# An encoder layer's last projection, moved behind all gated projections and written as a 2x2 block product with seven multiplications

## The chip, the core and the metric

The kernel runs on one core of one Trainium2 chip. The metric is the time of one execution on the device, in microseconds (us). Smaller is better. Three runs of the kernel before took 2499.37, 2503.11 and 2503.69 us; their median is 2503.11 us.

The engines are named as the profile names them: PE does matrix multiplications (PEld loads their stationary operand), DVE is the vector engine, ACT the scalar engine, POOL is GpSimd, SP issues most transfers. PE adds into banks of PSUM; everything else lies in SBUF or in DRAM.

## What is computed

The layer works on two inputs x of 1024 rows by 1024 channels each (one prompt, one sample). It ends so:

```
y_f = (fz * silu(fg)) @ w_fourier_out
y_h = (z * silu(hg)) @ w_hyena_out
g_f, g_h = split(sigmoid(mg + b_merge))
out = (g_f * y_f + g_h * y_h) @ w_out
return x + rmsnorm(out, g_post)
```

All matrices there are 1024x1024 in float32. Each operand of a multiplication is split into a rounded part h and a rest l, and a product is h*h + h*l + l*h: three passes of PE. Only the last projection, `@ w_out`, and what feeds it are changed.

## The kernel before, in words

**Stages.** `phase_fourier` and `phase_main` compute the Fourier and the Hyena branch. `phase_gates` (L956) computes the rest of the gate columns of x1 @ w_in. `phase_out` (L1066) does the two output projections, the merge and the last projection.

**How phase_gates multiplies.** It writes a product as 2x2 blocks, with Winograd's form of seven block products in place of eight. A job is one pair of 128-column blocks of w_in: `prepare` (L964) loads four 128x512 pieces by POOL's queue into two buffers "raw", and DVE and ACT make the sums s1 to s4 and split everything. `times` (L1011) is one block product: 12 matmuls of 128x512. The seven are named by their left operand: 11, 12, s2, s3, s1, s4, 22. Some add into the same PSUM bank: 11, then s2, then s1, then s4 all go into `pa`, and ACT copies the bank to SBUF (`kept`, L1034) between them. So a product into `pa` has to wait until the copy of the one before is done. The next job's 11 and 12 stand between this job's s1 and s4.

**How phase_out works.** A unit is one half (512 rows) of one input: four units. For each unit:
- f: eight products `pyf` (L1105, one for each 128 output channels, 24 matmuls each), times the sigmoid gate (`gated`, L1114), giving `yf`;
- h: eight products `pyh`, gated and added to `yf`. The sum is the operand of the last projection, `M`; ACT and DVE split it into `mh` and `ml`, which stay in SBUF;
- out: four row tiles of 128 rows by 1024 columns, `po`: 2 x 24 matmuls each, with `M` as the stationary and w_out as the moving operand. ACT squares `po` and sums it, DVE multiplies by g_post, `rstd` (L232, a chain of small DVE operations) and a multiply-add with x give the output rows.

The operands of f and h are tiles `sf` and `sh` (`operand`, L1078), 256 KB each, loaded by SP's queue into the places of the split x (`xh`, `xl`), and split by ACT and DVE. The weights of f and h stream through POOL's queue (`weight`, L1092): 128x512 pieces in three buffers, two of the pool `wp` and one of `op`, each loaded, split and used for 12 matmuls. w_out is loaded in unit 0 (`load_wo`, L1123) between the f products, 16 pieces of 256 KB, split as they come and kept.

**What sets the order.** The program is put in order by a scheduler that works from its own times; every engine and every queue then runs its instructions strictly in that order, and each waits for its semaphores at its turn. An instruction that waits holds up all behind it on the same engine. `keep_in_program_order` pins the first matmul of a block product. `tc.issue_after` puts DMA issues behind a named instruction. A pool's buffers are reused in turn (`bufs`), and a tile may be written only when the last reader of its place is done; pools opened later in a stage take the places of pools of the stage before.

Of the kernel before, what the change touches and what calls it, by code (L numbers as in the profile page):

```python
# [16 lines left out]
P = 128  # L17
D = 1024
# [143 lines left out]
class K:  # L162
# [34 lines left out]
    def setup(self, ctx):  # L197
# [27 lines left out]
        self.d_g = [{s: [dt(f"d_g{b}_{s}_{k}", [P, L]) for k in range(8)] for s in (0, 4, 5, 6)} for b in range(NB)]  # L225
        self.d_w = [[[dt(f"d_w{s}_{k}_{i}", [P, L]) for i in range(2)] for k in range(8)] for s in range(3)]
        self.d_sh = [[dt(f"d_sh{b}_{k}", [P, L]) for k in range(8)] for b in range(NB)]

# [721 lines left out]


    PLAIN = [(5, 0), (5, 1), (6, 0), (6, 1), (5, 2), (5, 3), (6, 2), (6, 3), (5, 4), (5, 5)]

    def phase_gates(self):
# [6 lines left out]
        with ExitStack() as es:  # L961
# [29 lines left out]
            A = prepare(*jobs[0])  # L991

            TH, TL = [], []
            for k in range(4):
                r = gr.tile([P, 4, 512], F32, tag="raw", name="xraw", bufs=2)
                for i in range(2):
                    nc.sync.dma_start(r[:, 2 * i:2 * i + 2].rearrange("p a b -> p (a b)"), self.d_x[b][k + 4 * i])
                s = gw.tile([P, 4, 512], F32, tag="sum", name="xsum", bufs=1)
                self.sub("dve", s[:, 0::2], r[:, 0:2], r[:, 1::2])
                self.stt("dve", s[:, 1], s[:, 0], -1.0, r[:, 3], MUL, SUB)  # L1000
                self.add("dve", s[:, 3], s[:, 1], r[:, 2])
# [7 lines left out]
            T1, T2, T3, T4 = [[(TH[k][:, j], TL[k][:, j]) for k in range(4)] for j in range(4)]  # L1009

            def times(p, A, B, first):  # L1011
                for k in range(4):
                    h, l = A[0][:, k], A[1][:, k]
                    for j, (w, x) in enumerate(((h, B[k][0]), (h, B[k][1]), (l, B[k][0]))):
                        m = self.mm(p, w, x, first and k + j == 0, k + j == 5, True)
                        if k + j == 0:
                            tc.keep_in_program_order(m)

# [15 lines left out]
            def kept(p, own=False):  # L1034
                t = gw.tile([P, 512], F32, tag="u", name="u", bufs=1) if own else wp.tile([P, 512], F32, tag="w", name="m", bufs=2)
                nc.scalar.copy(t, p)
                return t

            def first(A):
                pa, pb = self.psum("mm", 4, "pg"), self.psum("X", 2, "pg")  # L1040
                times(pa, A["11"], B11, True)
                m1 = kept(pa)
                times(pb, A["12"], B21, True)
                return pa, pb, m1
            pa, pb, m1 = first(A)
            for i, (sec, c) in enumerate(jobs):
                out(sec, c, 0, pb, m1, ADD)
                times(pa, A["s2"], T2, False)
                u = kept(pa, True)
                pc = self.psum("T", 2, "pg")  # L1050
                times(pc, A["s3"], T3, True)
                times(pa, A["s1"], T1, False)
                v = kept(pa)
                out(sec, c + 1, 1, pc, v, SUB)
                last = (A, pa, pc, u)
                if i + 1 < len(jobs):
                    A = prepare(*jobs[i + 1])
                    pa, pb, m1 = first(A)
                A_, pa_, pc_, u = last
                times(pa_, A_["s4"], B22, False)  # L1060
                out(sec, c, 1, pa_, None, None)
                times(pc_, A_["22"], T4, False)
                out(sec, c + 1, 0, pc_, u, SUB)


    def phase_out(self):  # L1066


# [3 lines left out]
        with ExitStack() as es:  # L1072
            pool = lambda n: es.enter_context(tc.tile_pool(name=n, bufs=1, reuse_waits="tile"))
            oc, sp, op, ox = pool("oc"), pool("sp"), pool("op"), pool("ox")
            wo = {}
# [38 lines left out]
            def gated(i, dt, ps, sec, bias, out):  # L1114
                b, half = units[i]
                g = wp.tile([P, 512], F32, tag="gt", name="g", bufs=3)
                nc.sync.dma_start(g, self.d_g[b][sec][dt][:, 512 * half:512 * half + 512])
                nc.scalar.activation(g, g, AF.Sigmoid, bias=self.bm[:, bias:bias + 1])
# [3 lines left out]

            def load_wo(k):  # L1123
                wo[k] = [oc.tile([P, D], F32R, tag=f"{t}{k}", name=f"{t}{k}", bufs=1) for t in ("woh", "wol")]
                for n in range(2):
                    s = slice(512 * n, 512 * n + 512)
                    r = wp.tile([P, 512], F32, tag="gt", name="wor", bufs=3)
                    nc.sync.dma_start(r, a["w_out"][k * P:(k + 1) * P, s])
                    self.split(wo[k][0][:, s], wo[k][1][:, s], r, "dve", "act")

            S = {(0, "f"): [operand(0, "f", k) for k in range(8)]}
            gp = oc.tile([P, D], F32, name="gp")
            nc.sync.dma_start(gp, a["g_post"][0].partition_broadcast(P))
            for i, (b, half) in enumerate(units):
                Yf, M = [], []
                S[i, "h"] = []
                for dt in range(8):
                    ps = project(i, "f", "w_fo", dt, S[i, "f"])
                    S[i, "h"].append(operand(i, "h", dt))
                    if i == 0:  # L1140
                        load_wo(dt)
                    y = sp.tile([P, 512], F32, tag=f"ml{dt}", name=f"yf{dt}", bufs=1)
                    Yf.append(gated(i, dt, ps, 5, dt, y))
                S[i + 1, "f"] = []
                for dt in range(8):
# [4 lines left out]
                    self.add("dve", g, Yf[dt], g)  # L1150
                    mh = sp.tile([P, 512], F32R, tag=f"mh{dt}", name=f"mh{dt}", bufs=1)
                    ml = sp.tile([P, 512], F32R, tag=f"ml{dt}", name=f"ml{dt}", bufs=1)
                    self.split(mh, ml, g, "dve", "act")
                    M.append((mh, ml))
                for tt in range(4):
                    c = slice(P * tt, P * tt + P)
                    row = 512 * half + P * tt
                    x = ox.tile([P, D], F32, tag="x", name="xr", bufs=2)
                    nc.sync.dma_start(x, a[f"x{b}"][row:row + P, :])
                    ss = op.tile([P, 2], F32, tag="ss", name="ss", bufs=2)  # L1160
                    s1 = op.tile([P, 1], F32, tag="s1", name="s1", bufs=2)
                    rs = op.tile([P, 1], F32, tag="rs", name="rs", bufs=2)
                    ps = [self.psum("mm", 4, f"po{n}") if tt < 2 else self.psum(("X", "T")[n], 2, f"po{n}")
                          for n in range(2)]
                    o = ox.tile([P, D], F32, tag="o", name="o", bufs=2)
                    for n in range(2):
                        s = slice(512 * n, 512 * n + 512)
                        for k in range(8):
                            self.mm3(ps[n], (M[k][0][:, c], M[k][1][:, c]), (wo[k][0][:, s], wo[k][1][:, s]),
                                     k == 0, k == 7)  # L1170
                        sq = op.tile([P, 512], F32, tag="sq", name="sq", bufs=1)
                        nc.scalar.activation(sq, ps[n], AF.Square, accum_out=ss[:, n:n + 1])
                        self.mul("dve", o[:, s], ps[n], gp[:, s])
                    nc.vector.tensor_tensor(s1, ss[:, 0:1], ss[:, 1:2], op=ADD)
                    self.rstd(op, rs, s1, 1)
                    for n in range(2):
                        s = slice(512 * n, 512 * n + 512)
                        self.stt("dve", o[:, s], o[:, s], rs, x[:, s], MUL, ADD)
                        nc.sync.dma_start(a[f"y{b}"][row:row + P, s], o[:, s])

# [79 lines left out]
```

## Time and profile before

| | |
|---|---|
| median of three runs | 2503.11 us |
| the profiled execution | 2505.81 us |
| its span, first to last instruction | 2504.0 us |
| PE busy | 2432.6 us, 97%, 13280 matmuls |
| DVE busy | 1906.1 us, 76% |
| ACT busy | 1067.9 us, 43% |
| POOL busy | 465.6 us, 19% |
| mean DMA rate | 163 GB/s |
| `po` matmuls | 768, in four stretches between 2028 and 2495 us |

How to read it: a matmul record of 128x512 is 0.389 us long, but a new one starts every 0.2267 us, since they are pipelined; so PE's work is counted by the distance of starts. Idle time "<-" names what ended it. The granted clock is the share of full TensorE clock.

### The profile page before, as it was taken

The numbers are of one execution on the slowest core, as the hardware profiler recorded it, in microseconds if no ns is written. First come the engines' busy times: TensorE is split into PE (matmuls) and PEld (weight loads), VectorE is DVE, ScalarE is ACT, GpSimd is POOL, SyncE is SP. The second block draws the span as 40 slices with busy tenths as digits, with TensorE's granted clock in tenths as the row PEclk, the third lists the DMA queues.
The fourth block names the chain that finished last, engine by engine and source line by source line (L and its number), as shares of the span: only waits on it lengthen the run. The fifth ranks groups of instructions, "written<-read, shape, count | busy, mean of one in ns | idle before, by whom it ended". The sixth has DMA issues, their size and how long they took to land.

```text
span 2504.0 us, 37217 instructions
## 1 busy us (share of the span) xinstructions
PE 2432.6 (97%) x13280; PEld 2106.1 (84%) x13280; DVE 1906.1 (76%) x3719; ACT 1067.9 (43%) x2000; POOL 465.6 (19%) x482
## 2 busy tenths in 40 slices
PE   6999999999999999999999999999999999999998
PEld 6988888888878888888888888887888778888887
DVE  7686788888788999999889999976655564545444
ACT  6546666666643333333323323323433552424241
POOL 1331222222233433440000001212000110101010
PEclk9999999999999999999999999999999999999999
DMA  7636555555555555546444443434454763545441
GB/s 270 200 105 220 195 162 163 157 171 163 172 183 179 178 170 163 175 145 210 127 136 133 135 144 127 148 127 168 160 181 133 246 218 122 188 136 173 146 144 51
DMA packets 204945, 408.40 MB, mean 163 GB/s; under 512 B 22662, under 2 KB 69991, under 8 KB 204376
## 3 DMA queue, kind: packets, MB, share of 16 engines
q1 hardware_dynamic: 180252, 319.71, 39.5%
q0 software_dynamic: 24320, 86.31, 10.1%
q8 instruction: 104, 1.70, 0.3%
q14 instruction: 81, 0.66, 0.1%
q10 hardware_dynamic: 188, 0.02, 0.0%
HBM read 280.11 MB, written 125.83 MB: 162 GB/s over the span
## 4 chain that ended last, share of the span: by engine, by line
PE 46%; DMA 5%; DVE 2%; issue 1%; ACT 1%; SPq 0%; DVEq 0%; POOL 0%; ACTq 0%; POOLq 0%
PE pin L194 13%; PE pg L194 8%; PE po L194 6%; PE pyf L194 5%; PE pyh L194 5%; PE pT L194 4%; PE pX L194 4%; DMA g<-d_g 1%; DMA sf<-d_g 1%; PE tph L783 1%; DMA xraw<-d_x 1%; DMA wr<-in_w_fo 1%; DMA wraw<-in_w_in 0%; DMA sh<-d_g 0%; DVE xsum L181 0%
## 5 line engine op out<-in xcount | busy, mean ns | idle before, releaser
L194 PE MATMUL pin<-xh,wh 128*128 128x512 f32 x1440 | 564.6, 393 | 3.6 <-DVE v L177 1.8
L194 PE MATMUL pin<-xh,wl 128*128 128x512 f32 x1440 | 564.2, 393 | 1.5 <-POOL wl L181 1.5
L194 PE MATMUL pin<-xl,wh 128*128 128x512 f32 x1440 | 564.8, 392 | 0.0
L181 POOL TENSOR_TENSOR wl<-wr,wh 128x512 fp32r<-128x512 f32 x132 | 251.1, 1902 | 1135.4 <-ACT wh L171 1083.6
L194 PEld LDWEIGHTS pin<-xh,wh 128*128 128x128 f32 x1440 | 271.7, 189 | 53.8 <-DVE v L177 2.0
L194 PEld LDWEIGHTS pin<-xh,wl 128*128 128x128 f32 x1440 | 271.6, 189 | 51.7 <-POOL wl L181 2.4
L194 PEld LDWEIGHTS pin<-xl,wh 128*128 128x128 f32 x1440 | 271.8, 189 | 49.6
L171 ACT CAST wh<-wr 128x512 fp32r<-128x512 f32 x260 | 159.7, 618 | 245.5 <-PE pin L194 110.6
L194 PE MATMUL pT<-cinv,yh 128*128 128x256 f32 x1024 | 194.2, 284 | 0.0
L194 PEld LDWEIGHTS pT<-cinv,yh 128*128 128x128 f32 x1024 | 166.7, 193 | 9.2
L181 DVE TENSOR_TENSOR t<-pX,k 128x1024 f32<-128x1024 f32 x128 | 155.4, 1214 | 11.1 <-PE pX L194 7.5
L194 PE MATMUL pyh<-sh,wh 128*128 128x512 f32 x512 | 159.4, 393 | 2.0 <-ACT wh L171 2.0
L194 PE MATMUL pX<-bh,cfwd 128*128 128x256 f32 x768 | 160.4, 287 | 0.6 <-DVE t L181 0.6
L194 PE MATMUL pyf<-sf,wh 128*128 128x512 f32 x512 | 158.0, 390 | 0.0
L194 PE MATMUL pT<-cinv,yl 128*128 128x256 f32 x512 | 146.3, 286 | 4.8 <-DVE yl L181 4.8
L171 ACT CAST yh<-y 128x512 fp32r<-128x512 f32 x128 | 79.5, 621 | 158.2 <-DVE y L181 125.6
L171 ACT CAST bh<-b 128x512 fp32r<-128x512 f32 x144 | 88.6, 618 | 119.5 <-DVE b L181 81.4
L194 PEld LDWEIGHTS pX<-bh,cfwd 128*128 128x128 f32 x768 | 125.5, 191 | 3.9 <-DVE t L181 1.0
L181 DVE TENSOR_TENSOR bl<-b,bh 128x512 fp32r<-128x512 f32 x144 | 110.3, 767 | 22.2 <-ACT bh L171 22.1
L181 DVE TENSOR_TENSOR wl<-wr,wh 128x512 fp32r<-128x512 f32 x128 | 87.4, 685 | 46.5 <-ACT wh L171 46.2
L194 PEld LDWEIGHTS pyh<-sh,wh 128*128 128x128 f32 x512 | 96.6, 189 | 23.1 <-ACT wh L171 3.2
L194 PEld LDWEIGHTS pyf<-sf,wh 128*128 128x128 f32 x512 | 96.1, 188 | 20.2
(307 smaller groups left out, 5342.1 us busy)
## 6 DMA issues: line engine op xcount, KB each, us to landing
k<-d_k SPq DMA_DIRECT2D x128, 512.0 KB, 4.0
wr<-in_w_in SPq DMA_DIRECT2D x132, 256.0 KB, 3.2
d_g<-gt SPq DMA_DIRECT2D x124, 256.0 KB, 2.4
d_k<-kt SPq DMA_DIRECT2D x128, 128.0 KB, 2.2
d_k<-kt SPq DMA_DIRECT2D x64, 256.0 KB, 2.3
wr<-in_w_fo POOLq DMA_DIRECT2D x64, 256.0 KB, 3.6
g<-d_g SPq DMA_DIRECT2D x64, 256.0 KB, 3.0
wr<-in_w_ho POOLq DMA_DIRECT2D x64, 256.0 KB, 3.2
```

Source lines behind the costliest of these rows:

```text
L171: self.rounded = nc.scalar.copy(h, src)
L181: e.tensor_tensor(out, a, b, op=op)
L194: return self.nc.tensor.matmul(out, lhsT, rhs, start=start, stop=stop, skip_group_check=shared)
L783: nc.tensor.transpose(tp[:, q * P:(q + 1) * P], eo[:, e, q], self.ident)
```

## The change

1. **The last projection comes after all four units** (`last_rows`). In h, DVE's merged `g` isn't split but written to DRAM (`d_m`, in segments of 512 B).
2. **It is a block product with seven multiplications**, as in `phase_gates`: eight jobs, each one pair of 128-row tiles, 7 x 12 = 84 matmuls. `prepare` reads two pieces of 512 KB from `d_m` through POOL's queue, makes the sums and splits them. The places of `sf` and `sh` hold the pieces.
3. **w_out is kept as blocks**: `blocks` loads it in four steps of 2 x 512 KB in unit 1 (two in f, two in h), splits three blocks and two sums, and writes the other two sums to DRAM (`d_t`); `sum1` and `sum4` read these back in units 2 and 3.
4. **Operands**: all eight `sf` go to the places xh0 to xh3 and xl0 to xl3, all `sh` to xh4 to xh7 and xl4 to xl7, where before four `sf` of unit 0 had places of their own.
5. **In phase_gates** the last job's s4 goes into a bank of its own (`pd`) and is added to the copy v, where before it added into `pa`.
6. **At the end** the last job does 22 ahead of s4 and finishes its two row tiles one by one; POOL does two of each job's four multiplications by g_post (a half row of 512 columns each).

The diff, cut to its core (`first`, `kept` and `times` of `last_rows` are as in `phase_gates`):

```diff
@@ phase_gates, per job
-                times(pa_, A_["s4"], B22, False)
-                out(sec, c, 1, pa_, None, None)
+                if i + 1 < len(jobs):
+                    self.times(pa_, A_["s4"], B22, False)
+                    out(sec, c, 1, pa_, None, None)
+                else:
+                    pd = self.psum("X", 2, "pg")
+                    self.times(pd, A_["s4"], B22, True)
+                    out(sec, c, 1, pd, v, ADD)
@@ phase_out
-                if nm == "f" and i == 0 and k >= 4:
-                    t = ox.tile([P, 2, 512], F32R, tag="xo"[k % 2], name=f"sf{k}", bufs=2)
-                else:
-                    t = xp.tile([P, 2, 512], F32R, tag=f"x{'l' if nm == 'h' else 'h'}{k}", name=f"s{nm}{k}", bufs=1)
+                t = xp.tile([P, 2, 512], F32R, tag=f"x{'hl'[k // 4]}{k % 4 + 4 * (nm == 'h')}", name=f"s{nm}{k}", bufs=1)
+            def blocks(k):
+                r = sc.tile([P, 4, 512], F32, tag="raw", name="oraw", bufs=1)
+                for i in range(2):
+                    nc.sync.dma_start(r[:, 2 * i:2 * i + 2].rearrange("p a b -> p (a b)"),
+                                      a["w_out"][(k + 4 * i) * P:(k + 4 * i + 1) * P])
+                s = sc.tile([P, 4, 512], F32, tag="sum", name="osum", bufs=1)
...
+                self.split(h[:, 0], l[:, 0], r[:, 0], "dve", "act")
+                self.split(h[:, 1:3], l[:, 1:3], r[:, 2:4], "dve", "act")
...
+                self.sums(s, r)
...
+                self.split(h, l, s[:, 1:3], "dve", "act")
...
+                for j in range(2):
+                    nc.sync.dma_start(self.d_t[j][:, k], s[:, 3 * j])
...
-                    if i == 0:
-                        load_wo(dt)
+                    with tc.issue_after(self.fetched.ins):
+                        if i == 1 and dt % 4 == 1:
+                            blocks(dt // 4)
+                        if i == 2 and dt == 3:
+                            sum1()
...
-                    self.split(mh, ml, g, "dve", "act")
-                    M.append((mh, ml))
-                for tt in range(4):
...
+                    nc.sync.dma_start(self.d_m[i][:, :, dt], g.rearrange("p (t c) -> p t c", t=4))
+                    if i == 1 and dt % 4 == 1:
+                        with tc.issue_after(self.fetched.ins):
+                            blocks(2 + dt // 4)
+                    if i == 3 and dt % 2 == 1:
+                        sum4(dt // 2)
@@ last_rows, new
+        jobs = [(u, t) for u in range(4) for t in (0, 2)]
+        def prepare(i):
+            u, t = jobs[i]
+            R = [xp.tile([P, 2, 512], F32, tag=g, name="mraw", bufs=1) for g in (("xl1", "xl2"), ("xl6", "xl7"))[i % 2]]
+            for j in range(2):
+                nc.gpsimd.dma_start(f(R[j]), self.d_m[u][:, t + j].rearrange("p a b -> p (a b)"))
...
+            for n, r in (("11", r0), ("12", r1)):
+                parts(n, r, *[wp.tile([P, 4, P], F32R, tag=t, name=t, bufs=2) for t in ("wh", "wl")])
...
+            def half_row(j, n, p, q, op2, eng):
...
+                if q is None:
+                    nc.scalar.activation(sq, p, AF.Square, accum_out=ss[:, j, n:n + 1])
+                    self.mul("dve", o[j][:, s], p, gp[:, s])
+                else:
+                    self.tt("dve", o[j][:, s], p, q, op2)
+                    nc.scalar.activation(sq, o[j][:, s], AF.Square, accum_out=ss[:, j, n:n + 1])
+                    self.mul(eng, o[j][:, s], o[j][:, s], gp[:, s])
...
+            half_row(0, 0, pb, m1, ADD, "pool")
+            self.times(pa, A["s2"], T2, False)
+            w = kept(pa, True)
+            pc = self.psum("T", 2, "po")
+            self.times(pc, A["s3"], T3, True)
+            self.times(pa, A["s1"], T1, False)
+            v = kept(pa)
+            half_row(1, 1, pc, v, SUB, "pool")
...
+            if i + 1 < len(jobs):
+                A = prepare(i + 1)
+                pa, pb, m1 = first(A)
...
+            if i + 1 == len(jobs):
+                pd = self.psum("mm", 4, "po")
+                self.times(pd, A_["22"], T4, True)
+                self.tt("dve", w, pc_, w, SUB)
+                half_row(1, 0, pd, w, ADD, "dve")
+                finish(1)
+            self.times(pa_, A_["s4"], B22, False)
+            half_row(0, 1, pa_, None, None, None)
+            if i + 1 < len(jobs):
+                self.times(pc_, A_["22"], T4, False)
+                half_row(1, 0, pc_, w, SUB, "dve")
+                finish(0, 1)
+            else:
+                finish(0)
```

More of the change, by code (lines that the diff above doesn't have):

```diff
@@ L226, in setup @@
         self.d_w = [[[dt(f"d_w{s}_{k}_{i}", [P, L]) for i in range(2)] for k in range(8)] for s in range(3)]
+        self.d_m = [dt(f"d_m{u}", [P, 4, 8, P]) for u in range(2 * NB)]
+        self.d_t = [dt(f"d_t{j}", [P, 4, 512]) for j in range(2)]
         self.d_sh = [[dt(f"d_sh{b}_{k}", [P, L]) for k in range(8)] for b in range(NB)]
@@ L949, in branches, with times, sums @@
                 self.spill_gate(1, sec, c, ws)
+    def times(self, p, A, B, first):
+        for k in range(4):
+            h, l = A[0][:, k], A[1][:, k]
+            for j, (w, x) in enumerate(((h, B[k][0]), (h, B[k][1]), (l, B[k][0]))):
+                m = self.mm(p, w, x, first and k + j == 0, k + j == 5, True)
+                if k + j == 0:
+                    self.tc.keep_in_program_order(m)
+    def sums(self, s, r):
+        self.sub("dve", s[:, 0::2], r[:, 0:2], r[:, 1::2])
+        self.stt("dve", s[:, 1], s[:, 0], -1.0, r[:, 3], MUL, SUB)
+        self.add("dve", s[:, 3], s[:, 1], r[:, 2])
     PLAIN = [(5, 0), (5, 1), (6, 0), (6, 1), (5, 2), (5, 3), (6, 2), (6, 3), (5, 4), (5, 5)]
@@ L1009, in phase_gates @@
             T1, T2, T3, T4 = [[(TH[k][:, j], TL[k][:, j]) for k in range(4)] for j in range(4)]
[L1011 to L1017, printed above, removed]
             def out(sec, c, n, p, q, op):
@@ L1035, in kept @@
                 t = gw.tile([P, 512], F32, tag="u", name="u", bufs=1) if own else wp.tile([P, 512], F32, tag="w", name="m", bufs=2)
-                nc.scalar.copy(t, p)
+                copied = nc.scalar.copy(t, p)
+                if own:
+                    self.copied = copied
                 return t
@@ L1040, in first @@
                 pa, pb = self.psum("mm", 4, "pg"), self.psum("X", 2, "pg")
-                times(pa, A["11"], B11, True)
+                self.times(pa, A["11"], B11, True)
                 m1 = kept(pa)
-                times(pb, A["12"], B21, True)
+                self.times(pb, A["12"], B21, True)
                 return pa, pb, m1
@@ L1073, in phase_out @@
             pool = lambda n: es.enter_context(tc.tile_pool(name=n, bufs=1, reuse_waits="tile"))
-            oc, sp, op, ox = pool("oc"), pool("sp"), pool("op"), pool("ox")
-            wo = {}
+            bl, sp, oc, sc, op = pool("bl"), pool("sp"), pool("oc"), pool("sc"), pool("op")
             self.nw = 0
@@ L1116, in gated @@
                 g = wp.tile([P, 512], F32, tag="gt", name="g", bufs=3)
-                nc.sync.dma_start(g, self.d_g[b][sec][dt][:, 512 * half:512 * half + 512])
+                self.fetched = nc.sync.dma_start(g, self.d_g[b][sec][dt][:, 512 * half:512 * half + 512])
                 nc.scalar.activation(g, g, AF.Sigmoid, bias=self.bm[:, bias:bias + 1])
@@ L1121, in gated @@
                 return out
[L1123 to L1131, printed above, removed]
+            BH, BL, TH, TL = [], [], [], []
@@ new lines, in blocks @@
+            def blocks(k):
[4 more added lines that the diff above has]
+                s = sc.tile([P, 4, 512], F32, tag="sum", name="osum", bufs=1)
+                h, l = [bl.tile([P, 3, 512], F32R, tag=f"{t}{k}", name=f"{t}{k}", bufs=1) for t in ("bh", "bl")]
+                self.split(h[:, 0], l[:, 0], r[:, 0], "dve", "act")
+                self.split(h[:, 1:3], l[:, 1:3], r[:, 2:4], "dve", "act")
+                BH.append(h)
+                BL.append(l)
+                self.sums(s, r)
+                h, l = [bl.tile([P, 2, 512], F32R, tag=f"{t}{k}", name=f"{t}{k}", bufs=1) for t in ("th", "tl")]
+                self.split(h, l, s[:, 1:3], "dve", "act")
+                TH.append(h)
+                TL.append(l)
+                for j in range(2):
+                    nc.sync.dma_start(self.d_t[j][:, k], s[:, 3 * j])
@@ new lines, in phase_out, with sum1, sum4 @@
+            T1, T4 = [], []
+            def sum1():
+                h, l = [sc.tile([P, 4, 512], F32R, tag=t, name=n, bufs=1) for t, n in (("raw", "t1h"), ("sum", "t1l"))]
+                r = l.bitcast(F32)
+                nc.sync.dma_start(r, self.d_t[0])
+                for k in range(4):
+                    self.split(h[:, k], l[:, k], r[:, k], "dve", "act")
+                    T1.append((h[:, k], l[:, k]))
+            def sum4(k):
+                h, l = [sp.tile([P, 512], F32R, tag=f"yf{2 * k + j}", name=f"t4{'hl'[j]}{k}", bufs=1) for j in range(2)]
+                r = l.bitcast(F32)
+                nc.sync.dma_start(r, self.d_t[1][:, k])
+                self.split(h, l, r, "dve", "act")
+                T4.append((h, l))
@@ L1132, in phase_out @@
+            with tc.issue_after(self.copied.ins):
+                S = {(0, "f"): [operand(0, "f", k) for k in range(8)]}
             gp = oc.tile([P, D], F32, name="gp")
@@ L1134, in phase_out @@
             for i, (b, half) in enumerate(units):
-                Yf, M = [], []
+                Yf = []
                 S[i, "h"] = []
@@ L1150, in phase_out @@
                     self.add("dve", g, Yf[dt], g)
-                    mh = sp.tile([P, 512], F32R, tag=f"mh{dt}", name=f"mh{dt}", bufs=1)
-                    ml = sp.tile([P, 512], F32R, tag=f"ml{dt}", name=f"ml{dt}", bufs=1)
-                    self.split(mh, ml, g, "dve", "act")
-                    M.append((mh, ml))
-                for tt in range(4):
[L1156 to L1166, printed above, removed]
-                        s = slice(512 * n, 512 * n + 512)
[L1168 to L1179, printed above, removed]
@@ new lines, in phase_out @@
+                    nc.sync.dma_start(self.d_m[i][:, :, dt], g.rearrange("p (t c) -> p t c", t=4))
[4 more added lines that the diff above has]
+                        sum4(dt // 2)
+            block = lambda j: [(BH[k][:, j], BL[k][:, j]) for k in range(4)]
+            T = [[(TH[k][:, j], TL[k][:, j]) for k in range(4)] for j in range(2)]
```

75 lines of the change are left out of this document (67 added, 8 removed).

## The prediction

> **What bounds the kernel now.** First the page's list of engines and its chain by engine and by line.
>
> ```profile
> PE 2432.6 (97%) x13280; PEld 2106.1 (84%) x13280; DVE 1906.1 (76%) x3719; ACT 1067.9 (43%) x2000; POOL 465.6 (19%) x482
> ...
> PE 46%; DMA 5%; DVE 2%; issue 1%; ACT 1%; SPq 0%; DVEq 0%; POOL 0%; ACTq 0%; POOLq 0%
> PE pin L194 13%; PE pg L194 8%; PE po L194 6%; PE pyf L194 5%; PE pyh L194 5%; PE pT L194 4%; PE pX L194 4%; DMA g<-d_g 1%; DMA sf<-d_g 1%; PE tph L783 1%; DMA xraw<-d_x 1%; DMA wr<-in_w_fo 1%; DMA wraw<-in_w_in 0%; DMA sh<-d_g 0%; DVE xsum L181 0%
> ```
>
> PE is busy 97% of the span, so a matmul that goes is worth its full distance of starts, if nothing else is late. The chain in order of time, from the end of phase_gates, shows where that doesn't hold.
>
> ```profile
> 1947.86 5.49 DMA sf<-d_g
> 1953.43 0.63 ACT sf L171
> ...
> 1990.15 3.81 DMA wor<-in_w_out
> 1993.98 0.63 ACT woh L171
> 1994.77 0.40 issue
> 1995.25 0.68 DVE wl L181
> ...
> 2365.22 43.52 PE pyf L194 x192
> 2408.74 43.52 PE pyh L194 x192
> 2452.26 43.53 PE po L194 x192
> 2495.87 0.60 ACT sq L1172
> 2496.59 0.69 DVE o L181
> ```
>
> The last three stages are pure PE: 43.52 / 192 = 0.2267 us a matmul. At 1948 to 2020 the chain runs through loads and splits instead. What that cost is in PE's waits and in the windows (us; PE busy; ...; PEclk is the granted clock):
>
> ```profile
> PE pg L194 <- ACT m L1036: 3.8, 1, 3.8
> ```
> ```profile
> 1957.50:1961.50 4.00, 4.00 (x12) 3.10 (x11) 0.97 (x2) 0.94 (x2) 0.62 (x2) 0.57 0.93 284
> 2008.40:2019.50 11.10, 8.37 (x31) 5.43 (x32) 6.55 (x11) 7.03 (x14) 1.61 (x3) 1.00 0.91 306
> 2019.50:2023.00 3.50, 3.50 (x10) 2.73 (x9) 2.91 (x5) 1.60 (x3) 1.07 (x2) 0.52 0.83 328
> ```
>
> In the timeline PE's last matmul of s1 in phase_gates starts at 1952.54 and its last of all at 2495.39: 542.85 us for 2328 starts, which need 2328 x 0.2267 = 527.8. **So 15.1 us are lost.** By the starts: 5.7 at the last s4 of phase_gates (3.8 of waiting, then half clock), 6.8 in unit 0's f and h (the last two windows), 2.6 where `po` and h of later units begin. After the last matmul come 8.7 us of tail to 2504.0.
>
> **The change part by part.**
>
> *Matmuls.* `po` has 4 x 4 x 2 x 24 = 768 of them; the block product has 8 x 7 x 12 = 672, of the same 128x512 form as `pg`, whose records are 0.39 us like `po`'s. 96 x 0.2267 = **-21.8 us**. The order in which the built program's instructions stand on PE is the same up to phase_gates; then come 924 `pg`, four times 192 `pyf` and 192 `pyh`, and 672 `po`.
>
> *The last s4 (`pd`).* PE waited for the copy m, because ACT stood behind two loads of `sf` (5.3 us idle, "DMA sf<-d_g"). Those four loads were issued only at 1947.86; now all eight find their places free after the last job's product 11 and can go at 1934 to 1938, where their neighbours went. And s4 no longer waits for m. **-5.7.** Late next: the first weights of `pyf`. On ACT they now stand behind the split of sh4, whose load can go only when s4's second matmul has read its place (about 1953.6) and takes 5.5 us (sh<-d_sh, issues of this window) plus 0.6 and 0.6 of splits: 1960.1. PE gets there at 1952.5 + 25 x 0.2267 = 1958.2. **+1.9**, between 0 (a quick load) and 5.
>
> *w_out out of unit 0.* It removes 16 loads, 16 ACT splits (0.62) and 16 DVE splits (0.69) from the 64 us in which ACT and DVE were late; the chain goes through them. **-6.8**; left over: eight `sh` and eight `sf` loads still catch up there, **+1** (0 to 6.8).
>
> *w_out into unit 1.* 4 steps, each of 2.7 us on ACT (splits of 0.62, 1.06 and 1.06) and 5.8 us on DVE (sums of 1.23, 0.75 and 0.69; splits of 0.69, 1.23 and 1.23). In f a pair of products (10.9 us) asks DVE for about 2 x 2.8, in h for 2 x 3.5, so there is room; but each `oraw` of 512 KB is queued on SP behind (f) or between (h) eight operand loads of 256 KB, all released at once, and ACT's split of it stands ahead of weights that PE needs 13.6 us after the stage began. 2 MB + 1 MB + 0.3 MB at the 300 GB/s of the windows above are 11 us, plus 1.7 of splits, plus the weight's 1.3: 14. **+2.5** for both stages, from 0 to 6.8 (unit 0's price for the same bytes).
>
> *Operands of f and h.* `sh` of the next unit used to load during `po`; now it loads in the next f, ahead of its use by 43.5 us, and its splits stand between weights, as those of `sf` do in h now. Those h stages lost 0, 0.7 and 0. **+1.2** for three f stages. The -2.6 at the old `po` beginnings go with them (their wait was for `mh`, which isn't made any more).
>
> *`d_m`, out and back.* 32 writes of 256 KB on SP (d_g<-gt of the same size: 2.4 us) and 16 reads of 512 KB on POOL's queue (wraw: 5.9 us). In h, each write stands between two gate loads and frees the gate buffer for the third product on: load 3, sigmoid 0.7, wait, two DVE operations, 2.4 to 4 of writing are under 10 of 16.3 us. Hidden by the products. Job 0 reads what unit 0 wrote 300 us before; jobs 6 and 7 read unit 3's rows 100 us after. 0. One place has no such cover: job 1's two pieces, job 2's and two x tiles wait for the last `sh` and all start at the end E of h: 3 MB at 300 GB/s, 8 to 10 us. ACT has job 1's split ahead of the copy u that s1 of job 0 needs at E + 4 x 2.72 = E + 10.9; from landing to u there are 4.7 us of splits, sums and a square. Landing at E + 6 is in time, at E + 8 is 2 late. **+1.5** (0 to 5).
>
> *The steady jobs.* 19.0 us of PE each. DVE: 14 operations of 0.69, one of 1.23, four of 0.75, twelve small ones, 16.1; ACT 9.1; POOL two multiplications. 11 and 12 are split one job ahead, copies have 2.7 us or more. **+0.5** (rival 2 has the other end).
>
> POOL's two multiplications run beside DVE, which the trace before shows at 1721: one of DVE's 0.68 us operations took 1.79 while POOL ran.
>
> ```profile
> 1720.82 1.64 POOL L181 TENSOR_TENSOR wl<-wr,wh 128x512 fp32r<-128x512 f32 x1 [5.41 <-ACT wh L171]
> ```
> ```profile
> 1721.22 1.79 DVE L181 TENSOR_TENSOR s2l<-wsum,s2h 128x512 fp32r<-128x512 f32 x1
> 1722.94 0.68 DVE L181 TENSOR_TENSOR s4l<-wsum,s4h 128x512 fp32r<-128x512 f32 x1
> ```
>
> Twice 1.1 makes DVE 18.3 of 19.0. The Trainium skill, "GPSIMD Engine Reference", 1. Specifications, says that GpSimd's SBUF interfaces are shared with VectorE, which contends when its instruction has two SBUF inputs: the trace agrees here, and the rule speaks against giving POOL this work.
>
> *The tail.* After the last matmul: square, multiply, chain, two multiply-adds, as before; but DVE's order puts row 1's two multiply-adds (1.41) and some six small steps (1.1) ahead of row 0's. **+2.5** (0 to 3).
>
> *Half clock.* After the cluster of gaps in the second window, none above 1.73 us, the third window ran at 0.52: 1.6 us lost. The Trainium skill, "TensorE: Matmul & The Clock Gate", What's actually happening, has the clock halved only after at least one idle window of about 3.4 us; by it the new gaps cost nothing more and the sum stays; by the row each cluster costs 1.6 more, -24.2 with one. The row decides against so strict a reading; I left single gaps without it, since one of 2.0 us at 1746.8 was followed by full clock.
>
> *Ahead of phase_gates* POOL now loads two pieces of f's weights early, and its last six splits of phase_main stand behind DVE's split of one. It should be there by 1707.5, POOL's next was at 1708.7: 0 (to +2).
>
> **Sum:** -21.8 - 5.7 - 6.8 - 2.6 + 1.9 + 1 + 2.5 + 1.2 + 1.5 + 0.5 + 2.5 = **-25.8 us.** The profiled execution took 2505.81, 1.8 more than its span and 2.7 more than the median 2503.11; against it 2480.0, against the median **2477**, which I give.
>
> **The rivals.**
> 1. *The stalls move and stay.* w_out costs in unit 1 what it cost in unit 0 (6.8), the first weights 4, job 1's pieces 4: all 15 again. For it: the same bytes, the same strict queues, 0.91 of DMA share in the second window. Against: larger loads, later and in four steps. -21.8 + 2.5 = -19.3: 2484.
> 2. *DVE bounds the jobs.* With POOL's contention it has 0.7 us to spare, and it waits in order for the copy v, for casts, for s4. If that costs 1 to 2 us beyond the slack, 22 waits for the read of its bank, and 8 jobs cost 8 to 16 more: 2485 to 2493. Against: phase_gates with nearly the same prepare lost 2.7 us in its 11 jobs ahead of the last s4, by the starts all of it in the first.
> 3. *The same ring, worse: slower than before.* A wait that comes round each job (22 for DVE's read of `pc`, that for the copy v, that for casts waiting on PE) decides from 25.8 / 8 = 3.2 us a job, so from 22.3 us: above 2503, at 5 us a job 2517. Between 2.6 and 3.8 it looks like no change. Against: no cast in the order is needed by PE in less than 2.7 us.
> 4. *Nothing new is late:* -21.8 - 15.1 + 2: 2468.
>
> That fewer matmuls aren't run is excluded by the order.
>
> **How the numbers follow.** Forecast 0.55, rival 1 0.22, rival 2 0.11, rival 4 0.03, the ring at no change 0.03, slower 0.06. Range 2468 to 2494: from rival 4 to the end of rival 2, which also holds the unknown costs' bounds. 0.2% (5 us) is about what can be told from no change here: faster 0.91, same 0.03, slower 0.06.
>
> **What would show it.** PE's groups: 672 `po`, starts 0.2267 apart; 152 us from the first `po` to the last. No wait of `pg` for m; one wait of 1 to 3 us at the first `pyf`; no waits in unit 0; waits of `pyf` or `pyh` in unit 1 for `wh` or `wl` behind `bh`. Rival 2: `po` waits for DVE `o` in every job. The prediction is wrong if the jobs take over 20 us each, or if units 2 and 3 lose more than 2 us.

## The result, and the profile after

The changed kernel is slower: 2513.14 us, median of 5 runs (2508.86 to 2515.5), against 2502.71 (5 runs) of the kernel before: ratio 1.0044, 95% interval 1.003 to 1.0059. The profiled executions took 2513.14 and 2505.81 us, so where the sum said -25.8 the profiles say +7.3 (the medians +10.4): some 33 us are to be explained. The list of engines and the chain by engine and line, from the page of the changed kernel:

```profile
PE 2421.5 (96%) x13184; PEld 2086.3 (83%) x13184; DVE 1955.7 (78%) x3737; ACT 1097.8 (44%) x2043; POOL 495.8 (20%) x514
...
PE 47%; DMA 8%; DVE 3%; issue 1%; ACT 1%; SPq 0%; DVEq 0%; ACTq 0%; POOL 0%
PE pin L194 17%; PE pg L194 8%; PE po L194 6%; PE pT L194 5%; PE pX L194 5%; PE pyf L194 4%; DMA d_m<-g 2%; DMA oraw<-in_w_out 1%; PE pyh L194 1%; DMA g<-d_g 1%; PE tph L785 1%; DMA xraw<-d_x 1%; DVE g L181 1%; DMA sh<-d_g 1%; DMA sf<-d_g 1%
```

The 96 matmuls are gone (13280 to 13184). But the chain's DMA share rose from 5 to 8%, `pyh` fell from 4 to 1% because the chain leaves PE in h, and `d_m<-g` stands there with 2%: the write that the prediction costed at nothing. The gate load `g<-d_g` has 1%, as before. The chain in unit 2's h, in order of time, shows that write and load form a ring, work that comes round and waits for itself (start, us, what):

```profile
2214.45 3.72 DMA d_m<-g
...
2218.18 3.48 DMA g<-d_g
...
2222.39 0.61 ACT wh L171
...
2223.64 0.68 DVE g L181
...
2224.84 0.70 DVE g L181
...
2225.55 4.07 DMA d_m<-g
```

One turn goes from the write of product 0 to the write of product **2**, not 3. The gate load of product 3 takes the buffer that the write of product 0 still reads, so it waits for that write to land. On ACT the sigmoid of product 3 stands ahead of a weight split; on DVE the `wl` behind that split stands ahead of the multiply of product 2. SP's queue, ACT and DVE, same place (start, duration, engine, line, what; the last bracket is the idle time before and what ended it):

```profile
2218.18 0.32 SPq L1126 DMA_DIRECT2D g<-d_g  x1
2218.59 0.52 SPq L1196 DMA_DIRECT2D d_m<-g  x1
2223.69 0.32 SPq L1126 DMA_DIRECT2D g<-d_g  x1
```
```profile
2221.76 0.72 ACT L1127 ACTIVATE g<-g,bm 128x512 f32<-128x512 f32 x1 [6.00 <-DMA g<-d_g]
2222.39 1.12 ACT L171 CAST wh<-wr 128x512 fp32r<-128x512 f32 x2
```
```profile
2223.03 0.69 DVE L181 TENSOR_TENSOR wl<-wr,wh 128x512 fp32r<-128x512 f32 x1 [5.78 <-ACT wh L171]
2223.64 0.68 DVE L181 TENSOR_TENSOR g<-pyh,g 128x512 f32<-128x512 f32 x1
```

These gate loads are issued 3.7 (2214.45 to 2218.18) and 5.1 us after their writes, and ACT sits 6 us in front of weights. A turn takes 11.1 to 13.0 us, from the write of product 0 to that of product 6, for two products, which PE needs 10.9 for. The same buffers stop `po`: ms4 of job 0 takes a gate buffer that unit 3's next to last write still reads. DVE there, and the window behind it (length; busy us of PE, of its weight loads, of DVE, ACT and POOL; granted clock; DMA share; GB/s):

```profile
2347.74 0.69 DVE L181 TENSOR_TENSOR ms<-ms,mraw 128x512 f32<-128x512 f32 x1 [5.16 <-DMA d_m<-g]
```
```profile
2350.00:2355.50 5.50, 5.50 (x14) 4.24 (x14) 3.18 (x6) 1.13 (x3) 0.46 (x1) 0.51 0.68 191
```

PE stood 4.2 us and then ran 12 matmuls at half clock, 2.4 us more. From there on the last projection ran without a stop, 19.0 us a job as forecast; from its first matmul to its last it took 160.3 us, where the prediction had 152.

What each stage loses is worked out by the starts, as in the prediction: from the last start of the stage before it to its own last start, less 192 x 0.2267 us (672 for the new `po`). Us, one profiled execution each; "+ write", "pd alone" and the columns behind "after" are experiments told below ("both" is `ahead_paced`):

| stage | before | + write | pd alone | after | whole rows | blocks once | own tile | ahead | paced only | both | spread |
|---|---|---|---|---|---|---|---|---|---|---|---|
| last products of the gates | 5.7 | 3.2 | 2.3 | 0 | 0 | 0 | 0 | 0 | 0 | 0 | 0 |
| unit 0: f, h | 0.7, 6.1 | 2.6, 7.8 | 7.0, 2.8 | 4.1, 2.7 | 3.6, 5.3 | 3.2, 3.0 | 3.2, 0.5 | 3.1, 0.2 | 1.0, 0 | 1.5, 0.4 | 2.7, 0.4 |
| unit 1: f, h | 0, 0 | 0, 4.9 | 0, 0 | 5.9, 5.8 | 4.6, 5.2 | 3.3, 5.3 | 3.2, 4.8 | 2.0, 8.0 | 9.4, 3.3 | 6.8, 2.6 | 0, 0 |
| unit 2: f, h | 0, 0.7 | 0, 7.5 | 0, 0 | 8.3, 3.4 | 8.0, 5.0 | 8.3, 3.2 | 2.9, 0 | 0, 0 | 4.3, 0 | 1.2, 0.5 | 0.4, 0.4 |
| unit 3: f, h | 0, 0 | 0, 0.1 | 0, 0 | 1.1, 1.7 | 1.7, 3.0 | 1.1, 1.7 | 0, 3.2 | 0, 1.9 | 0, 2.0 | 0, 2.9 | 0.9, 2.1 |
| `po`, all | 1.9 | 8.2 | 0.2 | 8.2 | 6.1 | 7.1 | 1.8 | 1.8 | 2.1 | 1.9 | 1.8 |
| sum | 15.1 | 34.3 | 12.3 | 41.2 | 42.4 | 36.1 | 19.6 | 17.0 | 22.1 | 17.8 | 8.7 |

A profile is one execution of a kernel whose runs spread over several us. Those of "ahead", "both" and "blocks once" were 4 to 7 us faster than the medians, those of "before", "whole rows" and "paced only" 3 to 4 slower, and `own_tile`, profiled again, lost 16.2 in place of 19.6. So a difference of some 3 us between two columns can be chance.

So 26.1 us more are lost against 21.8 saved; phase_gates' first matmul came 2.0 later, its earlier jobs lost 0.4 less, and the tail is 1.2 longer. These make 7.1 of the 7.3. The 2.0 are no part of the change that I can name: among the kernels here that matmul started between 1744.1 and 1748.9.

### The profile page after: what moved, and what is told of

Read it like the earlier page. It is cut to its first block, busy times and chain, and to the rows that moved or that the text cites. A ratio compares the mean times of both kernels' runs of the same rounds, so it can differ in the third digit from the quotient of the medians.

```text
span 2511.3 us, 37263 instructions
## 1 busy us (share of the span) xinstructions
PE 2421.5 (96%) x13184; PEld 2086.3 (83%) x13184; DVE 1955.7 (78%) x3737; ACT 1097.8 (44%) x2043; POOL 495.8 (20%) x514
## 3 DMA queue, kind: packets, MB, share of 16 engines
q0 software_dynamic: 26624, 94.70, 11.1%
## 4 chain that ended last, share of the span: by engine, by line
PE 47%; DMA 8%; DVE 3%; issue 1%; ACT 1%; SPq 0%; DVEq 0%; ACTq 0%; POOL 0%
PE pin L194 17%; PE pg L194 8%; PE po L194 6%; PE pT L194 5%; PE pX L194 5%; PE pyf L194 4%; DMA d_m<-g 2%; DMA oraw<-in_w_out 1%; PE pyh L194 1%; DMA g<-d_g 1%; PE tph L785 1%; DMA xraw<-d_x 1%; DVE g L181 1%; DMA sh<-d_g 1%; DMA sf<-d_g 1%
## 5 line engine op out<-in xcount | busy, mean ns | idle before, releaser
L181 DVE TENSOR_TENSOR t<-pX,k 128x1024 f32<-128x1024 f32 x128 | 155.8, 1217 | 10.9 <-PE pX L194 7.5
L194 PEld LDWEIGHTS pyf<-sf,wh 128*128 128x128 f32 x512 | 95.9, 189 | 30.9 <-ACT wh L171 11.7
```

The costliest lines, as they stand in the source:

```text
L181: e.tensor_tensor(out, a, b, op=op)
L194: return self.nc.tensor.matmul(out, lhsT, rhs, start=start, stop=stop, skip_group_check=shared)
```

## The experiments

**Is it the gate buffer?** `own_tile` frees it at the add:

```diff
-                    self.add("dve", g, Yf[dt], g)
-                    nc.sync.dma_start(self.d_m[i][:, :, dt], g.rearrange("p (t c) -> p t c", t=4))
+                    self.add("dve", Yf[dt], Yf[dt], g)
+                    nc.sync.dma_start(self.d_m[i][:, :, dt], Yf[dt].rearrange("p (t c) -> p t c", t=4))
```

> The changed kernel with one edit: in h the sum is written into f's own tile Yf (one of eight, next written 87 us later) and d_m is written from there, so that the write holds no gate buffer any more. Nothing else differs; in unit 3 the loads of t4 now wait for that write instead. Theory A, the ring: in h the trace of the changed kernel shows d_m write (4.0 us), gate load (4.0), sigmoid, weight split, multiply and add coming round in 12.96 us for two products that need 10.88; without the write in the ring about 9 us are left, the h stages of units 0 to 2 lose under 1 us each (2.7, 5.8 and 3.4 in the changed kernel, 11.8 together), and the 4.4 us stop of po for the buffer of ms4 with its 2.4 us of half clock goes too: 2497, from 2492 to 2504. Theory B, the transfers themselves (bytes and full queues make the gate loads late): 2511 to 2515, the h stages as before. Theory C, SP's strict order (the gate load stands behind the write whether it holds its buffer or not): 2509 to 2515.

Measured: 2489.22 us (6 runs), ratio to before 0.9947 (0.9934 to 0.996). That is 24 us less than the changed kernel, and more than theory A's range allowed: units 0 and 2 lose 0.5 and 0 in h, `po` 1.8, and the f stages behind the late h stages gave back 9.2 more (unit 2's alone 5.4), which A had left out. SP's queue in unit 2's h:

```profile
2209.47 0.53 SPq L1196 DMA_DIRECT2D d_m<-yf  x1
2210.05 0.62 SPq L1126 DMA_DIRECT2D g<-d_g  x1
```

The load still stands behind the write in SP's order, but now 0.6 us behind it. B and C fall: bytes and order are the same. Unit 1's h still loses 4.8, so there something else stands ready behind the ring; and unit 3's h pays 3.2 (2.1 in the repeat) for t4, the sums that `sum4` reads back: in the chain each t4 load now waits for a write of Yf, and a weight split for the t4 split.

**Does the write alone do it?** The reverse, on the kernel before:

```diff
                     self.add("dve", g, Yf[dt], g)
+                    nc.sync.dma_start(self.d_m[i][:, :, dt], g.rearrange("p (t c) -> p t c", t=4))
```

> The kernel before, which computes and keeps all it did, with one thing added: each sum of h is also written to d_m from the gate's buffer (32 writes of 256 KB that nobody reads). Theory A, the ring (the write holds the gate buffer, and load, sigmoid, weight split, multiply, add and write come round in some 13 us for two products of 10.9): each of the four h stages loses 2 to 6 us where it lost 0 in units 1 to 3: 2515, from 2510 to 2524. Theory B, the bytes alone (8.4 MB more): 2502 to 2506. If the ring needs the new kernel's operand places or blocks as well: 2502 to 2504.

Measured: 2527.15 us (4 runs), ratio 1.0103 (1.009 to 1.0116): 25 us for 32 writes that nobody reads, beyond theory A's range. By the two profiles it is 21 us, 19 of them in the table. PE's waits:

```profile
PE pyh L194 <- ACT wh L171: 11.1, 10, 2.9
PE po L194 <- ACT mh L171: 5.8, 3, 2.8
```

In unit 1 the writes of products 0, 2 and 4 were issued at 2161.24, 2172.93 and 2184.78: 11.7 and 11.8 us a turn. The ring needs none of the new operand places and no blocks. It also reaches into `po`, where `mh` and its DVE partner wait behind it. Unit 3's h lost only 0.1, though its turns took 11.0 to 12.2 us. It has no `sf` of a next unit to load, and its first write came 7.6 us behind the stage's first matmul, against 11.3 in unit 1; these 3.7 us may be the slack that bore the turns, which was not tried.

**Is the write slow because it goes out in 512 B pieces?**

```diff
-        self.d_m = [dt(f"d_m{u}", [P, 4, 8, P]) for u in range(2 * NB)]
+        self.d_m = [dt(f"d_m{u}", [P, 8, 4, P]) for u in range(2 * NB)]
...
-                    nc.sync.dma_start(self.d_m[i][:, :, dt], g.rearrange("p (t c) -> p t c", t=4))
+                    nc.sync.dma_start(self.d_m[i][:, dt].rearrange("p t c -> p (t c)"), g)
...
-                nc.gpsimd.dma_start(f(R[j]), self.d_m[u][:, t + j].rearrange("p a b -> p (a b)"))
+                nc.gpsimd.dma_start(f(R[j]).rearrange("p (a b) -> p a b", a=8), self.d_m[u][:, :, t + j])
```

> The changed kernel with one edit: d_m is kept as 128 x 8 x 512, so that the write of a product goes out in whole rows of 2 KB and the read comes in pieces of 512 B, where the changed kernel has it the other way round. Theory A, the ring: if the write falls from 4.0 us to the 2.4 of d_g's writes, the ring comes down from 12.96 to about 11.4 us for two products against 10.88: the h stages give back some 8 us, and job 1's slower reads cost 0 to 3: 2507, from 2502 to 2511. Theory B, the transfers' bytes: 2511 to 2516. Theory C, the strict order with its wait for a landing: as A, half of it.

Measured: 2511.98 us, ratio 1.004 (1.0026 to 1.0054): no gain, as theory B had it, which `own_tile` refutes. Theory A's premise fell, not the ring: in the window 2200 to 2250 a write of whole rows took 3.8 us from issue to landing, against 4.1. The 2.4 us that I took from d_g's writes belong to another stage.

**What do w_out's blocks cost in unit 1?**

```diff
             def blocks(k):
+                if k:
...
+                    for l in (BH, BL, TH, TL):
+                        l.append(l[0])
+                    for j in range(2):
+                        nc.sync.dma_start(self.d_t[j][:, k], only[0][:, 3 * j])
+                    return
```

> The changed kernel, but w_out's blocks are loaded, summed and split for the first of the four pieces only; the other three products' operands are those of the first piece, and only their d_t writes are kept. So it leaves out 6 of 8 loads of 512 KB, 3 of 4 rounds of sums and splits. Theory A (the ring causes most of it, the blocks add their own): unit 1's stages lose 11.7 us in the changed kernel, of which the chain of waits lays 1.6 + 1.6 + 0.5 at the pieces' splits in f and 3.7 + 2.2 in h; the first piece's own 2.4 and its half clock stay, so 6 to 8 us go: 2506, from 2504 to 2509. Theory D (the blocks are the main cause of unit 1's and of unit 2's beginning): 12 to 18 us go, 2495 to 2501. If the ring alone binds there: 2510 to 2514.

Measured: 2508.93 us (8 runs), ratio 1.0027 (1.0014 to 1.0039): some 4 us less than the changed kernel, at the upper end of A's range. By the stages, f gave back 2.7 and h 0.5, while unit 2's 8.3 stayed. D falls. My reading is that with the ring in place two causes lie side by side in unit 1's h, and that taking one away frees little.

**What does `pd` give?**

```diff
-                times(pa_, A_["s4"], B22, False)
-                out(sec, c, 1, pa_, None, None)
+                if i + 1 < len(jobs):
+                    times(pa_, A_["s4"], B22, False)
+                    out(sec, c, 1, pa_, None, None)
+                else:
+                    pd = self.psum("X", 2, "pg")
+                    times(pd, A_["s4"], B22, True)
+                    out(sec, c, 1, pd, v, ADD)
```

> The kernel before with only the edit of phase_gates' last job: the last s4 goes to a bank of its own and v is added behind it; nothing of the last projection is changed. By my sum this takes away the 5.7 us at the last s4 and adds up to 1.9 at the first weights of pyf: 2499, from 2497 to 2501. The rival: the stall only moves to pyf, whose first weights stand behind the same loads on ACT: 2501 to 2504.

Measured: 2505.07 us (11 runs), ratio 1.0013 (1.0003 to 1.0023): nothing, or a little worse. The gates' end loses 3.4 less, unit 0's f 6.3 more and its h 3.3 less. In the chain, the write of a gate result (`d_g<-gt`, 7.6 us from 1961.60), w_out's loads and splits and, from 1979, f's gate loads take over at once. The rival holds, 1 us past its range: the stall moves. That ACT is late there by a fixed sum of loads, whichever matmul waits for it, is my reading and not shown.

**Where do the other 19.6 us sit?** Two versions of `own_tile` move loads away from their splits: in `ahead` w_out's pieces are fetched two products early, t1 three, and t4 is read a pair later; `paced_only` and `ahead_paced` put each `sh` behind its own product's gate:

```diff
-                        if i == 1 and dt % 4 == 1:
-                            blocks(dt // 4)
+                    if i == 1 and n % 4 == 0:
+                        fetch(n // 4)
+                    if i == 1 and n % 4 == 2:
+                        blocks(n // 4)
...
-                    S[i, "h"].append(operand(i, "h", dt))
                     y = sp.tile([P, 512], F32, tag=f"yf{dt}", name=f"yf{dt}", bufs=1)
                     Yf.append(gated(i, dt, ps, 5, dt, y))
+                    with tc.issue_after(self.fetched.ins), tc.issue_after(self.opened.ins):
+                        S[i, "h"].append(operand(i, "h", dt))
```

> The version with Yf as the written tile, and three moves of loads away from what reads them: w_out's pieces are loaded two products ahead of their splits and sums (which stand behind the sigmoid of that product), t1's load in unit 2 three products ahead of its four splits, which stand two products apart, and t4's loads one pair of products later. Nothing else is added or left out. Theory E (what is left in units 1 to 3, 3.2 + 4.8 + 2.9 + 3.2 us by the starts, is ACT's and DVE's splits standing in order behind a load just issued, ahead of weights): 9 to 13 us go: 2478, from 2476 to 2482. Rival (the load on DVE and ACT, or the bytes, cost it wherever they stand): only the 3.2 of unit 3 go: 2484 to 2488.

> The version with Yf as the written tile, and one move: each of the eight sh operands of an f stage is loaded and split behind its own product's gate, one by one, instead of all eight at the stage's beginning. Theory E (the split of an operand that is not needed for 40 us stands on ACT ahead of weights that are needed now): unit 0's f loses 3.2 us, unit 1's and 2's 3.2 and 2.9, part of these two by w_out and t1; 3 to 6 us go: 2485, from 2483 to 2487. Rival (the first weights are late by their own loads): 2488 to 2491.

> Both moves together on the version with Yf as the written tile: pieces of w_out, t1 and t4 loaded ahead, and sh paced. By theory E PE's losses from the last s4 to the end, 19.6 us with Yf alone, fall to 4 to 7: 2475, from 2472 to 2479. If the two moves hit the same stalls: 2477 to 2482. If their loads only push each other later: 2483 to 2489.

Measured: 2491.76, 2490.68 and 2492.01 us, ratios 0.9963 (0.995 to 0.9976), 0.9959 (0.9944 to 0.9974) and 0.9959 (0.9945 to 0.9973). None is clear of `own_tile`, and theory E falls as a whole. In part it may hold: unit 2's f went from 2.9 (1.6 in the repeat) to 0 with t1 ahead, unit 0's f from 3.2 to 1.0 with `sh` paced. But unit 1 lost 8.0, 10.0, 12.7 and 9.4: something in it costs that wherever its loads stand. What all four have in common is the burst. DVE of the changed kernel at the first piece:

```profile
2065.16 0.68 DVE L181 TENSOR_TENSOR wl<-wr,wh 128x512 fp32r<-128x512 f32 x1
2066.72 0.69 DVE L181 TENSOR_TENSOR bl<-oraw,bh 128x512 fp32r<-128x512 f32 x1 [0.88 <-ACT bh L171]
2067.65 1.23 DVE L181 TENSOR_TENSOR osum<-oraw 128x1024 f32<-128x1024 f32 x1 [0.24 <-DMA oraw<-in_w_out]
...
2071.13 1.29 DVE L181 TENSOR_TENSOR wl<-wr,wh 128x512 fp32r<-128x512 f32 x2
```

Between two `wl` lie 6 us; PE uses up half a weight in 12 x 0.2267 = 2.7. So the work was cut up: a piece in six steps, at most one to a product and behind that product's multiply, over 8 products from unit 0's h to unit 2's h, and t1 in unit 3 (against `ahead`):

```diff
-                    if i == 1 and n % 4 == 2:
-                        blocks(n // 4)
+                    if 12 <= n < 44:
+                        if n % 8 == 4:
+                            fetch((n - 12) // 8)
+                        elif n % 8 != 5:
+                            piece((n - 12) // 8, (n - 12) % 8)
```

> The version with Yf as the written tile, t4's loads a pair of products later, and the work on w_out's pieces cut up: each piece is loaded, and then split, summed and split again in six steps, at most one of them to a product, from unit 0's h to unit 2's h (8 products a piece); t1 is loaded and split in unit 3's f. Nothing is added or left out. Theory F (in the versions tried so far unit 1 loses 8 to 13 us wherever the loads stand, because a piece's 5.8 us on DVE in one burst are more than the 2.7 us by which a half weight is split ahead): unit 1 loses under 2 us, unit 2's f and unit 3's h about 2 together, so 8 to 11 us of the 19.6 go: 2480, from 2477 to 2483. Rival (the bytes or the total load on DVE, wherever they stand): the losses spread over units 0 to 2 and stay: 2486 to 2492.

> As spread, and each sh operand is loaded and split behind its own product's gate in f. Theory F with it: unit 0's f loses 1 to 1.5 instead of 3.2, the stages of units 1 and 2 stay under 1 each: 2478, from 2475 to 2481. If sh among the pieces' steps is what costs unit 1's f (9.4 and 6.8 in the two versions that had it): 2483 to 2490.

> The same kernel as own_tile, for a comparison on the same chip with the two others: 2489, from 2486 to 2492.

Measured on one chip: `spread` 2480.06 us, ratio 0.9919 (0.9906 to 0.9932); `spread_paced` 2482.53, 0.9923 (0.991 to 0.9936); `own_tile` again 2487.67, 0.9946 (0.993 to 0.9962). Unit 1 of `spread` and of the changed kernel, as windows:

```profile
2048.00:2135.00 87.00, 87.00 (x386) 72.03 (x385) 55.51 (x85) 43.55 (x72) 16.63 (x31) 1.00 0.77 251
```
```profile
2053.68:2152.23 98.55, 90.72 (x385) 72.10 (x383) 65.11 (x94) 47.82 (x75) 16.63 (x31) 0.98 0.78 253
```

PE does not stop once, at nearly the same rate of transfers, which speaks against the bytes. Theory F's number came out: against the repeat on its own chip `spread` gains 7.6 us, though the two intervals just touch. `spread` changes two things in unit 1, though: the steps are apart, and half of them lie outside (DVE has 85 operations there instead of 94). `blocks_once` helps to tell them apart. In f of unit 1 it has one piece, in one burst, and `spread` has one piece's worth of steps (first `blocks_once`, then `spread`):

```profile
2049.42:2096.21 46.79, 44.56 (x193) 35.66 (x192) 27.90 (x41) 24.25 (x38) 9.12 (x17) 1.00 0.78 251
```
```profile
2047.92:2091.44 43.52, 43.52 (x194) 36.04 (x192) 26.57 (x40) 22.46 (x37) 8.58 (x16) 1.00 0.73 244
```

DVE does nearly the same work in both, 60 and 61% of the time, but `blocks_once` loses 3.3 us, 2.2 of them in two gaps at the burst, and `spread` none. So the burst counts by itself. `blocks_once` also has the ring in its h stages, so this is no clean pair. `spread_paced` adds nothing: unit 0's f fell to 1.7, but unit 3's f and h lost 3.9 and 4.8, for which I have no cause; its profile was the slowest of its five runs, 4 us above their median.

## Why the prediction was wrong, step by step

The step that failed is **`d_m`, out and back**: "each write stands between two gate loads and frees the gate buffer for the third product on: load 3, sigmoid 0.7, wait, two DVE operations, 2.4 to 4 of writing are under 10 of 16.3 us. Hidden by the products", at a price of 0. Both numbers were off. The turn took 11.1 to 13.0 us and not under 10: writes took 3.7 to 5.1 and gate loads 3.5 to 5.0. The larger error was the time it may take. I counted buffers (three, so three products) and not the orders of ACT and DVE, which pull the sigmoid of the next product ahead of this one's multiply. That leaves two products, 10.9 us; in 16.3 us even the measured turn would have been hidden. So the ring's wait falls on weights. Taking the hold away gave 24 us; adding it to the kernel before cost 25. The sign that the prediction had set came too: units 2 and 3 lost 14.5 us, where 2 were to show it wrong. Of my rivals none had this ring: number 3 is a ring, but I looked for it in the jobs of `po`. The 0.06 for "slower" was too little for 32 writes whose cover was one subtraction.

The other terms:
- *Matmuls* -21.8: as forecast. The steady jobs ran at 19.0 us of PE each.
- *Last s4* -5.7 and *first weights* +1.9: the s4 stall went (0 lost), f's beginning lost 3.4 more. `pd` alone only moves the stall (12.3 against 15.1 lost in all, no gain in time), so the -5.7 was not a term of its own.
- *w_out out of unit 0* -6.8, left over +1: h of unit 0 went from 6.1 to 2.7, and to 0.5 without the ring. That is -5.6, near the forecast, and the ring took 2.1 of it back.
- *w_out into unit 1* +2.5 (0 to 6.8): 8.0 and, in the repeat, 6.3 without the ring. The landing of the pieces was costed; the 6 us between two `wl` were not, though the 5.8 us of DVE a step stood in the text.
- *Operands of f and h* +1.2: unit 2's f alone lost 8.3, and 2.9 (1.6 in the repeat) without the ring; that went with t1's 1 MB load moved, of which the sum had no term. t4's had none either; without the ring they cost unit 3's h 2 to 3. The -2.6 "at the old `po` beginnings" held 0.7 that unit 2's h had lost; `po` itself had lost 1.9.
- *Job 1* +1.5, *steady jobs* +0.5: `po` lost 1.8 without the ring and 8.2 with it. That 1.8 is near the 2.0 of the sum is luck: in `own_tile` it is lost at the first two matmuls of job 0, whose weight splits stand behind a split of t4, and from 2325.86 on nothing stops `po`. Job 1's pieces cost nothing.
- *Tail* +2.5: 1.2 (9.8 us after the last matmul's start, against 8.6).
- *Half clock*, not counted: 20 matmuls ran at 0.43 us a start, 4.0 us lost, where before had 14 and 2.8.
- *POOL beside DVE* (rival 2): in each job one 128x2 operation took 1.14 us beside POOL; the four multiply-adds took 0.69 each as ever. In another place DVE's `wl` ran beside a multiplication of POOL and kept its 0.69 us, while POOL's took 1.92, where the job's other one took 1.30. It never reached PE.

The idea of the change was sound by its own sum: `spread` does the same 672 matmuls with the same DRAM trip at 2480.06 us, 0.8% less than before and 3 us above the forecast. Its profile lost 8.7 us where the sum had put in 8.6, but that is partly luck: the parts differ (unit 1 lost nothing, unit 3's h 2.1).

## What to carry to other kernels

When a write is added, ask what its source buffer is needed for next, and follow that need through every in-order engine back to the write: the time a ring may take is set by how many products apart its ends stand in those orders, not by the number of buffers. Write from a tile that nobody wants soon. And look at the length of a burst of off-path work on the engine that prepares weights, against the lead of one weight, and not only at that engine's share of busy time: with DVE about 60% busy PE waited in one kernel here and did not in another that did the work in single steps.

## What the runs showed of the hardware

Neither the length of a gap nor the number of gaps tells when the granted clock halves. In the changed kernel PE's starts had gaps of 1.06, 1.21 and 1.58 us within 13 us, and the next 3.5 us ran at 0.51; a single gap of 3.70 us (3.3 idle) was followed by full clock; in `own_tile` a single gap of 2.62 us was followed by half clock. The changed kernel:

```profile
2072.00:2075.50 3.50, 3.50 (x9) 2.71 (x10) 2.76 (x4) 1.89 (x3) 1.52 (x3) 0.51 0.73 222
```
```profile
2118.00:2121.50 3.50, 3.50 (x16) 2.89 (x17) 3.50 (x7) 0.37 (x1) 0.82 (x2) 1.00 0.38 121
```

The clock records of the 13 traces here resolve it. In each, all changes of the granted clock lie on a grid of 3.413 us. Cut from 1940 us on at this grid, with idle counted as the distance of two starts beyond 0.2267 us, 17 windows at full clock were followed by half clock. They had 1.99 to 3.08 us idle; of the 2033 windows that were not, the idlest had 2.08. The cluster put 2.28 us into one window and the gap in `own_tile` 2.39; the gap of 3.70 us lay across a border, 1.98 before it and 1.62 behind. So in these traces it is the idle time within one window that counts, from about 2.0 us on.

The Trainium skill, "TensorE: Matmul & The Clock Gate", What's actually happening, asks for an idle window of about 3.4 us. The length agrees with the grid; but here a window that was idle for 2.0 of its 3.4 us was enough, and the measurement decides.
